# Sums of the first norm in the transposes' PSUM banks, six projections in six banks, and the relative bias by one product of eight rows with copies in DRAM

## The chip, the cores and the metric

The kernel runs on one core of a Trainium2 chip. The metric is the device time of one execution in microseconds (us), from launch to end, as the median of several runs. The engines work in parallel, each through its own queue in a fixed order: TensorE (PE; PEld is its weight load), VectorE (DVE), ScalarE (ACT), GpSimd (POOL) and SyncE (SP), which issues the DMAs.

## The reference

A two-layer decoder trunk on 1024 tokens of width 1024, all in float32. Layer 0 is a mixer with two groups of heads, layer 1 is latent attention; a SwiGLU FFN follows each. The change lies in layer 0, whose core is:

```python
h = rmsnorm(x, attn_norm[0])                 # y * rsqrt(mean(y*y) + eps) * gain
proj = h @ w_in                              # q_a, k_a, v_a (8 heads), q_b (8), k_b, v_b (2)
# group A, stick-breaking attention: weights are products of (1 - sigmoid) over the keys between
# group B, window of 128 keys:
rel = BLOCK + arange(BLOCK)[:, None] - arange(2 * BLOCK)[None, :]
bias = rel_bias_table[t5_bucket(rel)]        # 32 buckets x 8 heads, the same for every block
logits = where(valid, q_b @ k_b.T * d ** -0.5 + bias, -inf)
p = exp(logits - m); p = p / (sum(p) + exp(sink - m))
x = x + concat([o_a, o_b]) @ w_out
```

## The kernel before

Activations lie transposed (channels on the 128 partitions, tokens along the row) in two halves of 512 tokens. Every float32 matrix operand is split into a rounded part and its rest (`whi`, `wlo` for weights, `hh`, `hl` for the normed input), and each product is made of three passes (`mm3`, L237 to L239): `whi*hh`, `whi*hl`, `wlo*hh`. One projection of one half is 8 k-steps, so 24 products of 128x512, collected in one PSUM bank.

PSUM has eight banks. In this stage they are four tags of two: `mm` (projections), `z` (scores), `t` (transposes) and `o` (attention outputs).

The stage begins with `norm_in` (L353): it loads the 16 tiles of x, splits them (`hh` on ACT, L311; `hl` on DVE, L312), squares them and adds the squares up in two tiles for each half (L270 to L277). The two are added on DVE (`merge`, L910), and a product with a matrix of ones (L285 in `rstd`) sums over the partitions. Then ACT takes Ln and Exp (L289, L296; each needs its table loaded) and DVE makes three steps (L297 to L299) to the scale `r` of that half. The projections don't wait for `r`: it is multiplied in when a bank is emptied (`evac`, L514).

Then come the first six projections by a loop in `layer0_attention`: k, q and v of the first pair of heads, both halves each, in the order k half 0, q half 0, k half 1, q half 1, v half 0, v half 1. An emptied q or k is split again for the scores (casts on ACT, L522, L531, L532; subtractions of 64x512 on POOL, L523, L533, L534; q takes two subtractions, k four). An emptied v is differenced (DVE L657, L659, POOL L655), transposed (PE L370) and split (ACT L376, DVE L377).

After them `weave` lays the rest out by hand for PE: eight segments (four pairs of stick-breaking heads, then four pairs of windowed heads). Each is a list of steps (transposes L706, values L719, scores L686, two slots ahead), and each carries fillers: the projections of a later segment, cut in pieces of two k-steps. The fillers' declared weights set the pace: after slot i of n, the share i/(n-1) of the whole weight should have run. Segment 3's fillers are the bias (`bias_items`), then k, one q and v of the windowed heads.

Up to the first segment the program's order on every engine, and in the whole program the order on DVE, ACT, POOL and SP, is chosen by a scheduler at build time that replays the program with modelled times; a change at one place can so change the order at another.

The bias: for each of the eight heads DVE spreads the head's column of the table over 128 columns (L435), PE multiplies it with a one-hot matrix of 33x384 in float32 (L436), which gives the head's row of 384 biases on all 128 partitions, ACT copies it out (L438), and SP stores it to DRAM (L439). There it is read back with a row step one element shorter (L581), which shifts each row by one, into the tile that L596 adds to the scores.

Of the kernel before, what the change touches and what calls it, by code (L numbers as in the profile page):

```python
# [10 lines left out]
F32 = mybir.dt.float32  # L11
# [4 lines left out]
ALU = mybir.AluOpType  # L16
# [4 lines left out]
P = 128  # L21
D = 1024
# [3 lines left out]
HALF = 512  # L26
# [3 lines left out]
WLEN = 384  # L30
# [33 lines left out]
def once(fn):  # L64
    def g():
        fn()
        return
        yield
    return g


class Kernel:
# [203 lines left out]
        eng = nc.gpsimd if k in (2, 4) else nc.vector  # L276
        eng.tensor_tensor(accs[k % 2], accs[k % 2], out, ALU.add)  # L277

    def rstd(self, r, accs, n, scale=1.0, eps=None, eps_out=None):


        nc, dv = self.nc, self.nc.vector
        ps = self.bank("mm")
        for i, acc in enumerate(accs):
            nc.tensor.matmul(ps, self.ones, acc, start=i == 0, stop=i == len(accs) - 1)  # L285
        v = self.tmp("nv")
        t = self.tmp("nt")
        if eps is None:
            nc.scalar.activation(t, ps, AF.Ln, scale=1.0 / n, bias=self.eps)  # L289
            dv.tensor_scalar(v, ps, 1.0 / n, EPS, ALU.mult, ALU.add)  # L290
        else:
            dv.scalar_tensor_tensor(v, ps, 1.0 / n, eps, ALU.mult, ALU.add)
            nc.scalar.activation(t, v, AF.Ln)
        if eps_out is not None:
            dv.tensor_scalar(eps_out, ps, EPS / n, EPS * EPS, ALU.mult, ALU.add)
        nc.scalar.activation(r, t, AF.Exp, scale=-0.5, bias=self.log_q if scale != 1.0 else 0.0)  # L296
        dv.tensor_tensor(t, r, r, ALU.mult)  # L297
        dv.scalar_tensor_tensor(t, t, -0.5 / scale ** 2, v, ALU.mult, ALU.mult)
        dv.scalar_tensor_tensor(r, t, 1.5, r, ALU.add, ALU.mult)  # L299
        return r  # L300
# [46 lines left out]
    def norm_in(self, xsrc, g0, pool, tag, split=False, hook=None):  # L347
        act = [[None, None] for _ in range(NT)]
        rs = []
        for hf in range(2):  # L350
            accs = []
            srcs = []
            for k in range(NT):  # L353
                if hook:
                    hook(k, hf)
                srcs.append(xsrc(k, hf))
                act[k][hf] = self.split_act(srcs[k], k, hf, g0 + k)
                if not split:
                    self.stat_acc(accs, srcs[k], k)
            if split:  # L360
                for k in range(NT):
                    self.stat_acc(accs, srcs[k], k)
            rs.append(self.rstd(self.tl(pool, [P, HALF], F32, tag, 2), self.merge(accs), D))
        return act, rs

    def v_tokens(self, fv, hf, v):
# [51 lines left out]
    def bias_items(self):  # L418

        nc, a = self.nc, self.a
        box = {}

        def start():
            t = self.tl(self.atp, [P, 514], F32, "w", self.nw)
            box["oh"], box["tab"] = t[:33, :WLEN], t[:33, WLEN:WLEN + 8]
            nc.sync.dma_start(out=box["oh"], in_=a["c_onehot"])
            nc.sync.dma_start(out=box["tab"][:32], in_=a["rel_bias_table"])
            nc.vector.memset(box["tab"][32:33], 1.0)  # L430

        def rows(h):
            ps = self.bank("mm")
            lhs = self.tl(self.atp, [P, HALF], F32, "u", 3)[:33, :P]
            nc.vector.tensor_scalar(lhs, self.ones[:33], box["tab"][:, h:h + 1], None, ALU.mult)  # L435
            nc.tensor.matmul(ps[:, :WLEN], lhs, box["oh"], start=True, stop=True)  # L436
            t = self.tl(self.atp, [P, HALF], F32, "ev", 2)
            nc.scalar.copy(t[:, :WLEN], ps[:, :WLEN])  # L438
            nc.sync.dma_start(out=self.dram("bias", h, width=WLEN + 1)[:, :WLEN], in_=t[:, :WLEN])  # L439

        return [(0, once(start))] + [(1, once(lambda h=h: rows(h))) for h in range(8)]

    def drive(self, segments):

# [124 lines left out]
    def swa_steps(self, mi, kbox, vbox, qbox, done):  # L569
        nc = self.nc  # L570
        g = mi // 2
        box = {}

        def score(b):
            if b % 4 == 0:
                box["s", b // 4] = self.tl(self.atp, [P, 2, 4], F32, "sum", 3)
            if b == 0:
                box["b"] = self.tl(self.atp, [P, HALF], F32, "u", 3)
                for h in range(2):
                    rows = self.dram("bias", 2 * mi + h, width=WLEN + 1)  # L580
                    nc.sync.dma_start(out=box["b"][:, 256 * h:256 * h + 256],  # L581
                                      in_=bass.AP(rows.tensor, rows.offset + P - 1, [[WLEN, P], [1, 256]]))
            bias = box["b"].rearrange("p (h k) -> p h k", h=2)
            khs, kls = kbox["t"]
            kh, kl, qs = khs[g], kls[g], qbox["t"]
            z = self.bank("z")
            zv = z.rearrange("p (h k) -> p h k", h=2)
            o = P if b == NB - 1 else 0
            for h in range(2):
                for i, k in enumerate((kh, kl)):  # L590
                    nc.tensor.matmul(zv[:, h, :], qs[h][:, b * P:(b + 1) * P],
                                     k[:, b * P - o:b * P - o + 256], start=i == 0, stop=i == 1)
            pt = self.tl(self.atp, [P, 2, 257], F32, "w", self.nw)
            st = self.tl(self.atp, [P, 2], F32, "sst", 6)
            nc.gpsimd.tensor_copy(pt[:, :, 256], self.sinks[:, 2 * mi:2 * mi + 2])
            nc.vector.scalar_tensor_tensor(pt[:, :, o:256], zv[:, :, o:], 0.125, bias[:, :, :256 - o],  # L596
                                           ALU.mult, ALU.add)
            nc.vector.tensor_reduce(st, pt[:, :, o:], AX.X, ALU.max, negate=True)
            for h in range(2):
                nc.scalar.activation(pt[:, h, o:], pt[:, h, o:], AF.Exp, bias=st[:, h:h + 1],  # L600
                                     accum_out=box["s", b // 4][:, h, b % 4:b % 4 + 1])
            box["p", b] = pt, o
# [16 lines left out]
        def pv(b, nk, hi, lo):  # L619
# [15 lines left out]
            if b % 4 == 3:  # L635
                hf = b // 4
                self.normalise(box["s", hf].rearrange("p h b -> p (h b)"), hf, ot, "u", 3)
                done(hf, ot)

        return [([(0, lambda b=b: score(b))], [lambda b=b: part(b)], None) for b in range(NB)]  # L640

    def sb_values(self, fv, hf, box):
# [114 lines left out]
    def layer0_attention(self):  # L757
        nc, a = self.nc, self.a
# [3 lines left out]
        with self.pool("at") as self.atp, self.pool("ps", space=PSUM) as self.ps:  # L762
# [39 lines left out]
            def q_tiles(i):  # L802
                if i < 2:
                    qt.append(self.qk_tiles(2))
                return qt[i % 2]

            qs = [self.unit_items(self.stack_q, lambda i=i: q_tiles(i)) for i in range(4)]
            for i, tag in ((0, "z"), (2, "mm"), (1, "z"), (3, "mm"), (4, "z"), (5, "mm")):
                self.dtag = tag
                for _ in sb[0][0][i][1]():  # L810
                    pass
# [906 lines left out]
```

## Time and profile before

| what | us |
|---|---|
| median of 3 runs (lowest to highest) | 2478.38 (2477.58 to 2479.45) |
| the profiled execution | 2477.88 |
| its span, first to last instruction | 2476.1 |
| PE busy | 2320.3 (94%) |
| DVE busy | 1914.9 (77%) |
| ACT busy | 1232.4 (50%) |
| POOL busy | 970.2 (39%) |

1.8 us of the profiled execution lie around the span. PE is busy nearly all the time, but a busy PE can run at two clocks (1.2 and 2.4 GHz), which the column PEclk of the view by windows shows as a share of the higher. In a timeline a row gives its start, its duration, the engine, the line, what it writes and reads, and in brackets the engine's idle time before it and what ended that.

### The profile page before, as it was taken

Reading aid. Unit: us, or ns where it says so; the run is one execution under the profiler, and the core shown is the slowest. Engines: PE = TensorE matmul, PEld = TensorE weight load, DVE = VectorE, ACT = ScalarE, POOL = GpSimd, SP = SyncE. Lnnn points to the kernel's source line nnn. Section 1 sums busy time; section 2 is a strip of 40 time slices with the busy share of each in tenths; the row PEclk is TensorE's granted clock in tenths of the full one; section 3 lists DMA queues with packets and bytes.
Section 4 is the critical chain, followed back from the end, with each engine's and each line's share of the span. In section 5 each row is a group of like instructions: output and inputs, shape, how many; then the busy total and the mean of one; then the engine's idle time right before and its main releaser. Section 6 shows DMA issues by size and latency. Waiting matters only on the chain. (4 is left out here: it accounts for less than half of the span.)

```text
span 2476.1 us, 33778 instructions
## 1 busy us (share of the span) xinstructions
PE 2320.3 (94%) x11252; PEld 1907.3 (77%) x11252; DVE 1914.9 (77%) x2864; ACT 1232.4 (50%) x2469; POOL 970.2 (39%) x786
## 2 busy tenths in 40 slices
PE   7999998889999999999987999999989999999996
PEld 5777787777788888778766888887768888887784
DVE  6787776778577678899987888885587776678988
ACT  6555565645223334344665788775453223243453
POOL 5333232213977443433222323321135564434333
PEclk8999999999999999999998999999999999999998
DMA  3011125644445335453343111135334443355531
GB/s 121 26 44 39 65 95 183 200 162 145 132 158 177 100 111 170 145 173 125 112 127 96 50 62 62 52 118 204 100 106 166 162 153 106 116 159 156 170 104 71
DMA packets 167114, 298.64 MB, mean 121 GB/s; under 512 B 20667, under 2 KB 29340, under 8 KB 166940
## 3 DMA queue, kind: packets, MB, share of 16 engines
q1 hardware_dynamic: 166940, 296.49, 36.7%
q8 instruction: 88, 1.44, 0.2%
q14 instruction: 86, 0.70, 0.1%
HBM read 214.53 MB, written 81.36 MB: 119 GB/s over the span
## 5 line engine op out<-in xcount | busy, mean ns | idle before, releaser
L145 ACT CAST whi<-wa 128x512 fp32r<-128x512 f32 (+1 forms) x422 | 255.7, 607 | 457.4 <-PE mm L238 111.9
L146 DVE TENSOR_TENSOR wlo<-wa,whi 128x512 fp32r<-128x512 f32 (+1 forms) x422 | 343.2, 814 | 75.4 <-ACT whi L145 73.5
L178 POOL TENSOR_TENSOR wa<-s,wa 128x512 f32<-128x512 f32 (+1 forms) x66 | 94.3, 1428 | 255.4 <-DVE wlo L146 227.3
L201 POOL TENSOR_TENSOR s<-wb,wb 128x512 f32<-128x512 f32 (+1 forms) x66 | 93.6, 1418 | 203.9 <-DVE wlo L146 149.9
L1470 PE MATMUL z<-mk,mq 128*128 128x512 f32 (+2 forms) x576 | 148.8, 369 | 10.1 <-ACT w L1483 9.4
L146 DVE TENSOR_TENSOR wlo<-wb,whi 128x512 fp32r<-128x512 f32 (+1 forms) x136 | 135.6, 997 | 25.8 <-ACT whi L145 25.7
L145 ACT CAST whi<-wb 128x512 fp32r<-128x512 f32 (+1 forms) x136 | 82.3, 605 | 141.6 <-PE d L238 44.6
L237 PE MATMUL mm<-hh,whi 128*128 128x512 f32 x312 | 128.5, 412 | 1.6 <-ACT whi L145 1.6
L1483 ACT ACTIVATE w<-z,st 128x512 f32<-128x512 f32 (+3 forms) x192 | 110.7, 582 | 32.5 <-DVE st L1479 23.2
L1476 DVE TENSOR_REDUCE st<-z 128x1 f32<-128x512 f32 (+1 forms) x192 | 104.2, 549 | 28.9 <-PE z L1470 19.9
L238 PE MATMUL mm<-hl,whi 128*128 128x512 f32 x312 | 125.3, 402 | 0.0
L239 PE MATMUL mm<-hh,wlo 128*128 128x512 f32 x312 | 124.8, 400 | 0.0
L178 POOL TENSOR_TENSOR wa<-wa,wa 128x512 f32<-128x512 f32 (+1 forms) x68 | 105.3, 1549 | 43.9 <-issue 26.8
L398 DVE TENSOR_TENSOR ptl<-t,pth 128x512 fp32r<-128x512 f32 x160 | 108.0, 682 | 13.3 <-ACT pth L397 10.7
L934 POOL TENSOR_TENSOR c<-c,c 128x512 f32<-128x512 f32 x66 | 101.6, 1554 | 26.0 <-DVE c L1052 22.7
L1470 PEld LDWEIGHTS z<-mk,mq 128*128 128x128 f32 x576 | 93.6, 193 | 23.3 <-ACT w L1483 14.6
L178 POOL TENSOR_TENSOR wb<-wa,wb 128x512 f32<-128x512 f32 (+1 forms) x68 | 100.1, 1472 | 27.0 <-DMA wa<-w_gate 23.1
L397 ACT CAST pth<-t 128x512 fp32r<-128x512 f32 x160 | 90.6, 591 | 17.3 <-PE t L394 7.5
L394 PE MATMUL t<-ident,w 128*128 128x128 f32 x576 | 95.0, 277 | 1.3 <-ACT w L1483 1.2
L402 PE MATMUL mm<-pth,v 128*128 128x256 f32 x320 | 93.5, 309 | 1.4 <-ACT pth L397 1.2
L402 PE MATMUL mm<-ptl,v 128*128 128x256 f32 x320 | 87.8, 298 | 2.4 <-DVE ptl L398 2.0
L710 DVE TENSOR_TENSOR ptl<-t,pth 128x512 fp32r<-128x512 f32 x80 | 54.4, 683 | 40.6 <-ACT pth L709 40.2
(530 smaller groups left out, 7613.3 us busy)
## 6 DMA issues: line engine op xcount, KB each, us to landing
a<-c SPq DMA_DIRECT2D x120, 256.0 KB, 3.1
ld<-a SPq DMA_DIRECT2D x98, 256.0 KB, 3.6
wa<-w_gate SPq DMA_DIRECT2D x68, 256.0 KB, 2.6
wa<-w_up SPq DMA_DIRECT2D x68, 256.0 KB, 2.7
lone<-a SPq DMA_DIRECT2D x56, 256.0 KB, 3.4
wb<-w_gate SPq DMA_DIRECT2D x44, 256.0 KB, 3.2
wb<-w_up SPq DMA_DIRECT2D x44, 256.0 KB, 2.7
wa<-w_in SPq DMA_DIRECT2D x36, 256.0 KB, 2.7
```

The lines of the kernel that those rows point to most:

```text
L145: nc.scalar.copy(hi[:, :n], raw[:, :n])
L146: nc.vector.tensor_tensor(lo[:, :n], raw[:, :n], f(hi[:, :n]), ALU.subtract)
L178: sub = lambda o, x, y: nc.gpsimd.tensor_tensor(o, x, y, ALU.subtract)
L237: mm(ps, wh, xh, start=first, stop=False)
L238: mm(ps, wh, xl, start=False, stop=False)
L239: mm(ps, wl, xh, start=False, stop=last)
L398: nc.vector.tensor_tensor(lo, t, f(hi), ALU.subtract)
L402: nc.tensor.matmul(o[:, :256], vs, pt[:, j * 256:(j + 1) * 256], start=(kb == kb0 and j == 0 and i == 0), stop=(kb == NB - 2 and j == 1 an ...
L934: sub = lambda o, x, y: nc.gpsimd.tensor_tensor(o, x, y, ALU.subtract)
L1470: nc.tensor.matmul(z[:, :wd + ext], qq[:, q0:q0 + P], kk[:, k0 - ext:k0 + wd], start=y == 0, stop=y == 2 and x > 0)
L1476: nc.vector.tensor_reduce(st[:, x:x + 1], zs[x], AX.X, ALU.max, negate=True)
L1483: nc.scalar.activation(w[:, o:o + wd], zs[x], AF.Exp, bias=st[:, 2 * np_ - 2:2 * np_ - 1], accum_out=box[p]["s"][c // 2][:, 8 * x + j:8 * ...
```

## The change

Four things are changed in layer 0. The sums of the first norm go to a bank of tag `t` instead of `mm`, and the two tiles of squares aren't added on DVE first: both go through the product with ones. Of the six first projections the last two (v) go to the banks `o`, where before v half 0 took a `z` bank and v half 1 an `mm` bank. The bias of all eight heads is made by one product, with the table itself as the stationary operand, as eight rows of 384; those go to DRAM, and eight DMAs from DRAM to DRAM spread one row each over 128 rows. The rows are read back as before. The bias is now one filler of declared weight 1 with a pause inside, where before it was a start of weight 0 and eight of weight 1.

```diff
-    def rstd(self, r, accs, n, scale=1.0, eps=None, eps_out=None):
+    def rstd(self, r, accs, n, scale=1.0, eps=None, eps_out=None, tag="mm"):
-        ps = self.bank("mm")
+        ps = self.bank(tag)
...
-            rs.append(self.rstd(self.tl(pool, [P, HALF], F32, tag, 2), self.merge(accs), D))
+            rs.append(self.rstd(self.tl(pool, [P, HALF], F32, tag, 2), accs if split else self.merge(accs), D,
+                                tag="t" if split else "mm"))
...
+        def rows():
             t = self.tl(self.atp, [P, 514], F32, "w", self.nw)
+            oh, tab = t[:33, :WLEN], t[:33, WLEN:WLEN + 8]
+            nc.sync.dma_start(out=oh, in_=a["c_onehot"])
+            nc.sync.dma_start(out=tab[:32], in_=a["rel_bias_table"])
+            nc.vector.memset(tab[32:33], 1.0)
+            yield
             ps = self.bank("mm")
+            nc.tensor.matmul(ps[:8, :WLEN], tab, oh, start=True, stop=True)
             t = self.tl(self.atp, [P, HALF], F32, "ev", 2)
+            nc.scalar.copy(t[:8, :WLEN], ps[:8, :WLEN])
+            rows = self.drp.tile([8, WLEN], F32, name=self.nm("bias"))
+            nc.sync.dma_start(out=rows, in_=t[:8, :WLEN])
+            self.bias = self.drp.tile([8, P, WLEN + 1], F32, name=self.nm("bias"))
+            for h in range(8):
+                nc.sync.dma_start(out=self.bias[h, :, :WLEN],
+                                  in_=bass.AP(rows.tensor, rows.offset + h * WLEN, [[0, P], [1, WLEN]]))
-        return [(0, once(start))] + [(1, once(lambda h=h: rows(h))) for h in range(8)]
+        return [(1, rows)]
...
-            for i, tag in ((0, "z"), (2, "mm"), (1, "z"), (3, "mm"), (4, "z"), (5, "mm")):
+            for i, tag in ((0, "z"), (2, "mm"), (1, "z"), (3, "mm"), (4, "o"), (5, "o")):
```

The change moves instructions at three places that the prediction speaks of. The first is PE at the end of the first norm. In the names, `z104` is the bank of k half 0, `mm114` of q half 0, `z116` of k half 1, `mm118` of q half 1; `mm97` and `t55` are banks of the norm's sums, `w46`, `w47` and `w88` tiles of squares. PE before, where the second half's sum stands:

```order
L237 MATMUL z116_372<-hh7_186_247,whi32_129 128x512
L238 MATMUL z116_372<-hl7_187_248,whi32_129 128x512
L239 MATMUL z116_372<-hh7_186_247,wlo33_130 128x512
L285 MATMUL mm97_275<-w88_251,ones3_62 128x512
L237 MATMUL mm114_341<-hh0_020_105,whi59_193 128x512
L238 MATMUL mm114_341<-hl0_021_106,whi59_193 128x512
```

PE now, from the last product that has its old place:

```order
L237 MATMUL z104_292<-hh7_044_153,whi32_129 128x512
L237 MATMUL mm114_341<-hh0_020_105,whi59_193 128x512
L238 MATMUL mm114_341<-hl0_021_106,whi59_193 128x512
L285 MATMUL t55_180<-w46_157,ones3_62 128x512
L237 MATMUL z116_372<-hh0_162_199,whi17_99 128x512
L237 MATMUL mm118_407<-hh0_162_199,whi59_193 128x512
L285 MATMUL t55_180<-w47_159,ones3_62 128x512
L238 MATMUL z104_292<-hl7_045_154,whi32_129 128x512
L239 MATMUL z104_292<-hh7_044_153,wlo33_130 128x512
L239 MATMUL mm114_341<-hh0_020_105,wlo60_194 128x512
```

Before, q half 0 stood behind the sum of the second half; now it is woven with k half 0, k half 1 and q half 1, and the sum of the second half (`t97`) comes 68 rows later than `t55`, between the last products of q half 1 and the first of v.

The second place is ACT around the second half's Ln (L289). ACT before (`ev105` is k half 0, `ev115` q half 0, `ev117` k half 1, emptied):

```order
L532 CAST qk100_288<-ev105_317 64x512
L531 CAST qk101_289<-ev105_317 64x512
L532 CAST qk101_289<-ev105_317 64x512
L289 ACT_TABLE_LOAD
L289 ACTIVATE w99_278<-mm97_275,eps7_70 128x512
L296 ACT_TABLE_LOAD
L296 ACTIVATE r096_273<-w99_278 128x512
L522 CAST qk112_339<-ev115_366 64x512
```

ACT now:

```order
L145 CAST whi110_335<-wa109_333 128x512
L524 CAST qk112_339<-ev115_366 64x512
L524 CAST qk113_340<-ev115_366 64x512
L145 CAST whi121_440<-wa120_438 128x512
L145 CAST whi124_446<-wa123_444 128x512
L289 ACT_TABLE_LOAD
L289 ACTIVATE w99_278<-t97_274,eps7_70 128x512
L296 ACT_TABLE_LOAD
L296 ACTIVATE r096_273<-w99_278 128x512
L533 CAST qk100_288<-ev117_397 64x512
```

The split of q half 0 has moved ahead of the second half's Ln, and with it four casts of later weights; the tag `whi` has four buffers, so `whi124` takes that of `whi68`, which the last product of q half 1 reads.

The third place is PE in segment 3. PE before, in the slots after the first pair of bias products (`o` values, `t` transposes, `z` scores):

```order
L686 MATMUL z_2750<-qk_1996,qk_2225 128x384
L686 MATMUL z_2750<-qk_1998,qk_2225 128x384
L436 MATMUL mm_2756<-w_2700,u_2757 128x384
L436 MATMUL mm_2764<-w_2700,u_2765 128x384
L719 MATMUL o_2772<-pth_2696,v_2436 128x256
```

PE now:

```order
L433 MATMUL mm_2704<-w_2700 8x384
L721 MATMUL o_2643<-pth_2653,v_1720 128x256
L721 MATMUL o_2643<-ptl_2654,v_1720 128x256
L721 MATMUL o_2643<-pth_2653,v_1720 128x256
L721 MATMUL o_2643<-ptl_2654,v_1720 128x256
```

Of eight bias products one is left (8x384), and the projections of k, q and v begin two slots after it and are spread over the whole segment, where before they began behind the eighth bias product. Beyond this the scheduler's order differs at a few rows near 490 us and, with the same instructions, in the first pairs of layer 1's attention (some 1315 to 1440 us in the trace of before).

## Rows read from the trace of the kernel before

**Rows 1.** The page's head and its first part: the span, and PE's busy time, share of the span and count.

```profile
span 2476.1 us, 33778 instructions
PE 2320.3 (94%) x11252; PEld 1907.3 (77%) x11252; DVE 1914.9 (77%) x2864; ACT 1232.4 (50%) x2469; POOL 970.2 (39%) x786
```

**Rows 2.** PE's waits from 0 to 72 us: what waited, on what, us in total, times, longest.

```profile
PE mm L285 <- DVE w L910: 7.7, 1, 7.7
...
PE t L706 <- DVE v L377: 3.3, 1, 3.3
PE z L686 <- ACT w L688: 1.4, 1, 1.4
```

**Rows 3.** Timelines of PE, ACT and DVE from 18 to 49 us, single rows in order of time: start us, duration us, engine, line, operation, out<-in, shapes, and in brackets the idle time before it.

```profile
19.68 0.72 PE L237 MATMUL z<-hh,whi 128*128 128x512 f32 x2
...
38.32 0.68 DVE L514 TENSOR_TENSOR ev<-z,r 128x512 f32<-128x512 f32 x1
...
38.45 2.08 PE L285 MATMUL mm<-w,ones 128*128 128x512 f32 x2 [7.65 <-DVE w L910]
39.54 1.42 PE L237 MATMUL mm<-hh,whi 128*128 128x512 f32 x1
...
41.58 1.28 ACT L289 ACT_TABLE_LOAD   x1
42.87 0.69 ACT L289 ACTIVATE w<-mm,eps 128x512 f32<-128x512 f32 x1
...
44.87 0.63 ACT L296 ACTIVATE r<-w 128x512 f32<-128x512 f32 x1
...
46.99 0.69 DVE L299 SCALAR_TENSOR_TENSOR r<-w,r 128x512 f32<-128x512 f32 x1
...
48.22 0.68 DVE L514 TENSOR_TENSOR ev<-z,r 128x512 f32<-128x512 f32 x1
```

**Rows 4.** Timeline of POOL from 28 to 80 us: the subtractions of k half 0, q half 0, and the first and last row of k half 1 and q half 1.

```profile
39.73 1.26 POOL L533 TENSOR_TENSOR qk<-ev,qk 64x512 fp32r<-64x512 f32 x1 [4.28 <-ACT qk L531]
...
49.04 2.66 POOL L523 TENSOR_TENSOR qk<-ev,qk 64x512 fp32r<-64x512 f32 x2 [4.05 <-ACT qk L522]
51.77 1.29 POOL L533 TENSOR_TENSOR qk<-ev,qk 64x512 fp32r<-64x512 f32 x1
...
57.88 2.65 POOL L523 TENSOR_TENSOR qk<-ev,qk 64x512 fp32r<-64x512 f32 x2
```

**Rows 5.** Timelines of PE and DVE from 52 to 72 us: the first and last product of v half 0, the first scores, the first transposes of segment 0, and the emptying of v half 1.

```profile
52.86 0.39 PE L237 MATMUL z<-hh,whi 128*128 128x512 f32 x1
...
58.07 0.39 PE L239 MATMUL z<-hh,wlo 128*128 128x512 f32 x1
...
63.75 0.63 PE L686 MATMUL z<-qk,qk 128*128 128x256 f32 x4
...
71.14 0.45 PE L706 MATMUL t<-ident,w 128*128 128x128 f32 x1 [3.32 <-DVE v L377]
...
64.00 0.69 DVE L514 TENSOR_TENSOR ev<-mm,r 128x512 f32<-128x512 f32 x1 [1.66 <-PE mm L239]
```

**Rows 6.** Busy time by windows: the window, then its length, busy us (and count) of PE, PEld, DVE, ACT, POOL; then PEclk, the share of the DMA engines, GB/s.

```profile
24.00:27.00 3.00, 3.00 (x7) 1.67 (x6) 3.00 (x6) 1.24 (x2) 0.00 (x0) 0.55 0.35 113
27.00:31.00 4.00, 3.80 (x17) 2.82 (x15) 4.00 (x7) 3.14 (x6) 0.00 (x0) 1.00 0.04 6
...
38.40:43.70 5.30, 5.25 (x10) 3.52 (x11) 0.71 (x2) 4.56 (x7) 3.80 (x3) 0.50 0.00 0
43.70:52.80 9.10, 9.10 (x41) 7.51 (x40) 3.88 (x6) 6.11 (x9) 4.90 (x4) 1.00 0.01 2
```

**Rows 7.** Timeline of DVE from 12 to 40 us: the same subtraction of a weight, once beside a square on POOL, once alone.

```profile
13.86 1.52 DVE L146 TENSOR_TENSOR wlo<-wa,whi 128x512 fp32r<-128x512 f32 x1
...
23.92 0.68 DVE L146 TENSOR_TENSOR wlo<-wa,whi 128x512 fp32r<-128x512 f32 x1
```

**Rows 8.** Timeline of PE from 272 to 300 us, the rows of the bias products (two records a product), and two of PE's waits from 272 to 345 us.

```profile
275.95 2.93 PE L436 MATMUL mm<-w,u 33*128 33x384 f32 x4
...
282.20 1.79 PE L436 MATMUL mm<-w,u 33*128 33x384 f32 x4
...
285.02 1.55 PE L436 MATMUL mm<-w,u 33*128 33x384 f32 x4
...
288.43 0.91 PE L436 MATMUL mm<-w,u 33*128 33x384 f32 x2
...
290.38 0.91 PE L436 MATMUL mm<-w,u 33*128 33x384 f32 x2
...
PE t L706 <- DVE w L690: 1.6, 1, 1.6
PE t L562 <- DVE ev L514: 1.3, 1, 1.3
```

**Rows 9.** The views by line of L439 (the time to landing of its eight DMAs of 128x384), L581 and L596: line, engine, operation, count, then ns min/median/max, first and last start in us, forms.

```profile
DMA to landing us min/median/max: 2.1/2.4/2.6
...
L581 SPq DMA_DIRECT2D u<-bias x8: 319/430/587, 286.6 to 459.9; - x8
...
L596 DVE SCALAR_TENSOR_TENSOR w<-z,u x32: 426/693/694, 344.8 to 488.6; 128x512 f32<-128x512 f32 x28, 128x256 f32<-128x256 f32 x4
```

**Rows 10.** PE's longest wait from 1300 to 1440 us, in the first pairs of layer 1's attention.

```profile
PE z L1470 <- ACT w L1483: 7.6, 4, 3.4
```

More of the change, by code (lines that the diff above doesn't have):

```diff
@@ L422, in bias_items @@
         nc, a = self.nc, self.a
-        box = {}
-        def start():
+        def rows():
             t = self.tl(self.atp, [P, 514], F32, "w", self.nw)
[L427 to L432, printed above, removed]
+            oh, tab = t[:33, :WLEN], t[:33, WLEN:WLEN + 8]
[3 more added lines that the diff above has]
+            yield
             ps = self.bank("mm")
-            lhs = self.tl(self.atp, [P, HALF], F32, "u", 3)[:33, :P]
-            nc.vector.tensor_scalar(lhs, self.ones[:33], box["tab"][:, h:h + 1], None, ALU.mult)
-            nc.tensor.matmul(ps[:, :WLEN], lhs, box["oh"], start=True, stop=True)
+            nc.tensor.matmul(ps[:8, :WLEN], tab, oh, start=True, stop=True)
             t = self.tl(self.atp, [P, HALF], F32, "ev", 2)
-            nc.scalar.copy(t[:, :WLEN], ps[:, :WLEN])
-            nc.sync.dma_start(out=self.dram("bias", h, width=WLEN + 1)[:, :WLEN], in_=t[:, :WLEN])
-        return [(0, once(start))] + [(1, once(lambda h=h: rows(h))) for h in range(8)]
+            nc.scalar.copy(t[:8, :WLEN], ps[:8, :WLEN])
[6 more added lines that the diff above has]
+        return [(1, rows)]
     def drive(self, segments):
@@ L579, in score @@
                 for h in range(2):
-                    rows = self.dram("bias", 2 * mi + h, width=WLEN + 1)
                     nc.sync.dma_start(out=box["b"][:, 256 * h:256 * h + 256],
-                                      in_=bass.AP(rows.tensor, rows.offset + P - 1, [[WLEN, P], [1, 256]]))
+                                      in_=bass.AP(self.bias.tensor, self.bias.offset + (2 * mi + h) * P * (WLEN + 1) + P - 1,
+                                                  [[WLEN, P], [1, 256]]))
             bias = box["b"].rearrange("p (h k) -> p h k", h=2)
```

## The prediction

> **What bounds the kernel now.** I read the page's busy times first: PE is busy 2320.3 of 2476.1 us, 94% [rows 1], so time can come only from work that PE no longer does where it is full, or from the few places where PE waits. Hence the view of PE's waits at the start, where three of the four edits lie: its longest is L285, 7.7 us for `merge` on DVE [rows 2]. The timelines around it [rows 3] show the chain behind: PE has had nothing to do since 38.45 - 7.65 = 30.80, DVE is late with the squares, and the sum of the second half starts at 38.45. From there nothing is parallel: table and Ln on ACT from 41.58, table and Exp until 45.50, three steps on DVE until 47.68, k half 1 emptied until 48.90, then the splits on POOL, which POOL takes one after another until 60.53 [rows 4], and the first scores at 63.75 [rows 5]. The windows show a second price of the wait: in the 5.3 us after it PE's clock is 0.50, thereafter 1.00 [rows 6]. So POOL's splits of k half 1 and q half 1 release the first scores, and they wait for the second half's scale.
>
> Last I read PE around segment 3: busy without a gap worth naming, apart from 1.6 and 1.3 us of transposes waiting, and the bias products stand in the middle of it [rows 8].
>
> **The start: 6.8 us, the likeliest gain.** With the sums in a bank of their own tag, PE need not hold q half 0 back. By the order it has issued 22 of the four projections' 96 products when it comes to the row at 19.68 [rows 3]; 74 are left. A product at full clock takes (58.07 - 52.86)/23 = 0.227 us [rows 5], so 16.8. Three products with ones (two for the first half, the first for the second) stand among them; one takes 39.54 - 38.45 = 1.09 [rows 3], so 3.3. From 19.7, with 0.4 for the last to drain, they end at 19.7 + 16.8 + 3.3 + 0.4 = 40.2. The squares of the second half were ready at 38.45 minus a merge, so the sum follows at once and DVE no longer sets it.
>
> Then the old chain, with durations of [rows 3]. On ACT stand a cast of a weight that waits for the last product of q half 1 (0.6, taken as Exp's on the same 128x512), table 1.28, Ln 0.69, table 1.28, Exp 0.63: 4.5, to 44.7. From the end of Exp (45.50) to the end of L299 (47.68) it took 2.2: to 46.9. Emptying k half 1 adds 0.7: 47.6, against 48.90 before. ACT's cast of it takes 0.6, so POOL begins at 48.2. It needs 60.53 - 51.77 = 8.8 for k half 1 and q half 1 [rows 4]: the first scores at 57.0, against 63.75. The larger part of the gain is thus not the 1.3 us by which the scale comes sooner: before, q half 0's 2.66 on POOL (49.04) stood ahead of k half 1 [rows 4], since q half 0 was computed behind the sum; now it is done before the scale is there. PE still has 48 products of v and one with ones in that time, 48 x 0.227 + 1.1 = 12.0, so it is through at 52.2, 4.8 us ahead of the scores, and POOL is the bound. What is late next is v half 1, emptied beside the first scores as before (64.00 [rows 5]). From the first scores to the first transposes 7.4 us pass (63.75 to 71.14 [rows 5]), and I leave them.
>
> The v banks themselves cost nothing I can find: a bank of `o` is first wanted by the values of segment 0, behind the transposes at 71.14; its cover is some 10 us after PE's 52.2. The merges that go (two on DVE) stood in front of the wait and are in the 7.7. The two products with ones that are new cost 2.2 and are in the sum above.
>
> Bounds: 74 products at the low clock (0.50 from 38.4 to 43.7 [rows 6]) would take twice as long, 33.6 instead of 16.8: scores at 73.8, 10.1 later than before. Of lower prices, a stretch like that from 24 to 27 us, granted 0.55 after PE had waited [rows 6], costs 3.0 x 0.45 = 1.4. At best the chain from scores to transposes also shortens by its 3.3 us wait for v [rows 2], and the gain is 9 to 10.
>
> A rule speaks against this term. The row first: the subtraction L146 of a weight takes 1.52 us beside a square on POOL and 0.68 alone [rows 7]. The Trainium skill (GPSIMD Engine Reference, section 1, Specifications) has GpSimd share SBUF interfaces with VectorE, and lose to contention where a VectorE instruction has two SBUF inputs; the trace agrees. Now k half 0's and q half 0's splits on POOL fall beside four weight subtractions and the last squares on DVE: by the rule 5 x 0.84 = 4.2 us more on DVE, of which I reckon that at most 2 reach the second half's sum, and the total would be 2 us higher.
>
> **The bias: 4.8 us.** The records of L436 add up to 2.93 + 1.79 + 1.55 + 0.91 + 0.91 = 8.09 us, two to a product, so seven products are 7.1 of it; at full clock one is 0.91 [rows 8]. I take seven at 0.91 as removed, 6.4. Against it one new wait like the 1.6 us of transposes for DVE [rows 8], since PE comes sooner to the same scans: 6.4 - 1.6 = 4.8. Nothing of the 8 steps on DVE and ACT counts, since PE doesn't wait for them except through the products. Bounds: zero, if what PE gains is lost at the next waits for DVE or ACT; 7.1 + 1.6 + 1.3 = 10, if waits vanish too.
>
> The eight copies from DRAM to DRAM, 196,608 bytes each, 1.57 MB in all, are in no row. The nearest are the eight stores of L439, which land 2.1 to 2.6 us after issue [rows 9]. One after another that would be 19 us. They are wanted when the loads L581 run ahead of the first L596, at 344.8 before and some 12 us sooner now, 333; the store before them comes with the product, near 270. So some 60 us cover them, and I cost them at nothing. All DMAs are issued by SP, in order: the first bias load waits for its copy, and behind it stand the weights of segments 4 on. If the cover is gone, PE waits for L596 and for those weights.
>
> By a page alone: the Trainium skill (DMA: Bandwidth & Descriptors, Anatomy of one DMA — SWDGE (gpsimd) path) fits 2.0 us and the bytes at 436 GB/s, on another path of issue; its estimate is 3.6 + 2.0 us, no run here shows it, and the sum would be the same.
>
> The even spread of segment 3's projections moves PE work within the segment and adds none: zero, inside the bounds above.
>
> **The reordered rows.** Near 490 us a few rows change places, and from 1315 to 1440 us whole pairs do, with the same instructions. PE's wait there is 7.6 us in four [rows 10], so one wait more or fewer is 1.9, two are 3.8. No row says which way: zero, plus or minus 3.8.
>
> **Sum.** 6.8 + 4.8 + 0 = 11.6. The profiled execution took 2477.88, its span 2476.1 and 1.8 around it, 0.5 below the median of 2478.38. So 2477.88 - 11.6 = 2466.3, and 2466.8 as a median.
>
> **Rivals.** Main case, 0.66: both gains come; 2466.8, of its own 2461 to 2472 (the reorder's 3.8, and 1 to 2 for the clock or POOL).
>
> The bias gain is hidden, 0.20: PE finds itself ahead of scans and softmax and waits there. For it: PE's waits before L706 [rows 8] all end on DVE. Against it: they are 2.9 us in 73. 2478.4 - 6.8 = 2471.6.
>
> The low clock holds through the start, 0.10: the woven products have gaps in them, and the clock stays at half. For it: PE busy 1.00 of the time at 0.55 from 24 to 27 us, and 0.50 after the long wait [rows 6]. Against it: the weave gives PE work that doesn't wait. The start would cost 10.1 instead of gaining 6.8: 2478.4 + 10.1 - 4.8 = 2483.7 at its worst; with half of the 74 products so, 8.4 of the 16.8 come on top, 2466.8 + 8.4 = 2475.2.
>
> Slower, 0.04: the copies hold SP. If 1.57 MB take more than about 60 us (25 GB/s), L596 waits for the bias and the weights behind it in SP's queue come late; the first 12 us of that only eat the gain, so it decides from about 73 us, 21 GB/s. At 78 us, 18 are lost: 2466.8 + 18 = 2484.8. For it: one row of 1536 bytes is read 128 times from DRAM. Against it: 2.4 us for as many bytes stored [rows 9].
>
> **Range and chances.** 2459 (both gains at their better bounds, with the reorder's) to 2477 (bias hidden, a low stretch, and the reorder against it). 0.2% is 5 us, about what a measurement of this kernel tells from no change: faster below 2473.4. All of the main case but a tenth, and most of the hidden one are faster, with some of the low clock: 0.78; the same 0.15; slower, from the worst of the low clock, of the copies and of the reorder, 0.07.
>
> **What would show it.** PE's wait at L285 for L910 is gone, and PE at 1.00 from 27 us until the v products end near 52; the first scores stand at 57, the first transposes of segment 0 near 64. POOL does q half 0 before k half 1. One L433 of about 0.9 us stands where eight L436 stood, and L596 starts near 333. The waits of layer 1 from 1300 to 1440 us stay near 7.6. I am wrong on the start if the scores come later than 62 with POOL idle before them or PE at 0.50 after 30; on the bias if PE's waits from 272 to the first L596 grow by more than 3; on the copies if L596 waits for a bias load longer than for any other.

## The result and the profile after

| what | us |
|---|---|
| before, median of 6 runs (lowest to highest) | 2478.82 (2477.58 to 2482.59) |
| after, median of 6 runs (lowest to highest) | 2466.96 (2461.47 to 2467.82) |
| ratio, with its 95% interval | 0.9948 (0.9935 to 0.9962) |
| after, the profiled execution and its span | 2461.47, 2459.7 |
| PE busy in it | 2311.8 (94%) |

The kernel became 11.9 us faster, where 11.6 were forecast. The profiled execution is the fastest of the six, 5.5 us below their median, so its end says less than its single stages; those are read here, and the same kernel was profiled once more below.

The start first. PE's waits from 0 to 72 us after the change, to be held against [rows 2]:

```profile
PE z L237 <- ACT hh L311: 6.0, 1, 6.0
PE z L688 <- POOL qk L525: 4.8, 1, 4.8
PE z L238 <- DVE hl L312: 3.8, 3, 2.0
PE t L708 <- DVE v L378: 1.2, 1, 1.2
```

The 7.7 us for `merge` are gone. In their place PE waits 4.8 us at the first scores, and what it waits for is the first of POOL's two last splits (L525). The timeline of PE after, single rows: the four sums, the last product of v half 1, the first scores, the first transposes of segment 0.

```profile
20.27 1.33 PE L285 MATMUL t<-w,ones 128*128 128x512 f32 x2
...
21.91 1.02 PE L285 MATMUL t<-w,ones 128*128 128x512 f32 x2
...
36.87 1.02 PE L285 MATMUL t<-w,ones 128*128 128x512 f32 x2
...
39.82 1.02 PE L285 MATMUL t<-w,ones 128*128 128x512 f32 x2
...
51.15 0.39 PE L239 MATMUL o<-hh,wlo 128*128 128x512 f32 x1
56.33 3.34 PE L688 MATMUL z<-qk,qk 128*128 128x256 f32 x8 [4.79 <-POOL qk L525]
...
64.11 0.45 PE L708 MATMUL t<-ident,w 128*128 128x128 f32 x1 [1.24 <-DVE v L378]
```

Against [rows 3] and [rows 5]: the last sum ran at 39.82 (the products ahead of it were put to end at 40.2), PE was through with v at 51.5 (52.2), the first scores stand at 56.33 (57.0; before 63.75) and the first transposes at 64.11 (64; before 71.14).

The scale itself came no sooner. DVE's timeline after, the first and last step of the scale (L297, L299) and the emptying of k half 1:

```profile
44.84 1.51 DVE L297 TENSOR_TENSOR w<-r 128x512 f32<-128x512 f32 x1 [0.96 <-ACT r L296]
...
47.11 0.69 DVE L299 SCALAR_TENSOR_TENSOR r<-w,r 128x512 f32<-128x512 f32 x1
47.90 0.69 DVE L516 TENSOR_TENSOR ev<-z,r 128x512 f32<-128x512 f32 x1
```

L299 ends at 47.80, in [rows 3] it ended at 47.68; 46.9 was put. Nearly all of these 0.9 us are L297's: it took 1.51 us beside POOL's split of q half 0 (42.80 to 45.79, below), where it had taken 0.69 before, with POOL idle. So what held the scores back in the kernel before? The view by windows of before, the stretch in front of them:

```profile
60.00:63.70 3.70, 3.70 (x18) 3.08 (x17) 0.69 (x1) 0.63 (x1) 1.71 (x3) 1.00 0.09 18
```

PE was busy all of it with the last products of v, while POOL had been done with its splits since 60.53 [rows 4]. Before, it was PE's own queue that stood in front of the first scores, late by the wait of 7.65 us and the low clock behind it; after, PE is through at 51.5 and POOL's splits stand there.

The clock, in the view by windows of after, answers to [rows 6]:

```profile
24.00:27.00 3.00, 3.00 (x15) 2.47 (x14) 3.00 (x6) 2.97 (x5) 0.00 (x0) 1.00 0.26 87
...
31.00:43.00 12.00, 12.00 (x51) 9.18 (x50) 11.16 (x10) 8.14 (x14) 9.17 (x7) 1.00 0.19 51
43.00:52.00 9.00, 8.54 (x38) 6.75 (x36) 5.06 (x7) 5.05 (x8) 5.29 (x4) 1.00 0.15 52
52.00:58.00 6.00, 1.62 (x5) 1.33 (x6) 2.97 (x4) 3.53 (x6) 5.74 (x4) 0.75 0.18 49
```

PE is busy without a gap from 24 to 51.5 us and the clock is 1.00 all the time; it falls only with the wait at the scores. POOL's timeline after is the chain that sets the scores, and shows the price of working beside DVE:

```profile
36.05 1.60 POOL L535 TENSOR_TENSOR qk<-ev,qk 64x512 fp32r<-64x512 f32 x1 [2.50 <-ACT qk L533]
37.71 1.64 POOL L536 TENSOR_TENSOR qk<-ev,qk 64x512 fp32r<-64x512 f32 x1
...
42.80 2.99 POOL L525 TENSOR_TENSOR qk<-ev,qk 64x512 fp32r<-64x512 f32 x2
49.33 1.29 POOL L535 TENSOR_TENSOR qk<-ev,qk 64x512 fp32r<-64x512 f32 x1 [3.53 <-ACT qk L533]
...
55.02 2.94 POOL L525 TENSOR_TENSOR qk<-ev,qk 64x512 fp32r<-64x512 f32 x2
```

q half 0 is split (42.80) ahead of k half 1 (49.33), as the sum had it; in [rows 4] it stood in front of it at 49.04. A subtraction takes 1.60 to 1.64 while DVE works beside it and 1.29 alone.

Segment 3 next. One and the same row of DVE near the segment's end, the rest of the windowed heads' values, bounds it. Before and after:

```profile
339.79 0.69 DVE L567 TENSOR_TENSOR v<-t,v 128x512 fp32r<-128x512 f32 x1 [1.37 <-ACT v L566]
```

```profile
327.34 0.67 DVE L569 TENSOR_TENSOR v<-t,v 128x512 fp32r<-128x512 f32 x1
```

That is 12.45 us sooner. At 247.41 before, a scan on DVE ahead of segment 3, the distance was 5.47, so the stretch between gained 7.0. PE's bias products in that stretch by the view by line, before and after (two records a product):

```profile
L436 PE MATMUL mm<-w,u 33*128 33x384 f32 x16 | 8.1, 624 | 0.0
```

```profile
L433 PE MATMUL mm<-w 33*8 33x384 f32 x2 | 1.4, 825 | 0.0
```

6.7 us of products are gone. And PE's waits in the stretch, before and after:

```profile
PE t L706 <- DVE v L377: 2.7, 1, 2.7
PE t L706 <- DVE w L690: 1.6, 1, 1.6
PE t L562 <- DVE ev L514: 1.3, 1, 1.3
...
PE t L370 <- DVE u L657: 0.6, 1, 0.6
```

```profile
PE t L708 <- DVE v L378: 2.3, 1, 2.3
PE z L688 <- ACT w L690: 1.9, 1, 1.9
PE t L371 <- POOL u L657: 0.6, 1, 0.6
PE t L371 <- DVE u L659: 0.6, 1, 0.6
```

The waits of 1.6 and 1.3 (both in [rows 8]) are gone, one of 1.9 for ACT is new: with the line left out (POOL, 0.6) the sums are 6.8 and 5.4. From there to the end the distance goes from 12.5 to 16.4 in this execution, in steps of one to three us up and down; the second profile below shows what to make of them.

The copies, SP's timeline of after: the store of the rows, the eight copies, the first two bias loads.

```profile
272.10 0.28 SPq L437 DMA_DIRECT2D bias<-ev  x1
273.52 5.05 SPq L440 DMA_DIRECT2D bias<-bias  x8
...
280.48 1.03 SPq L582 DMA_DIRECT2D u<-bias  x2
```

The loads go out at 280.48 and the first L598 stands at 330.36, 50 us later.

### The profile page after: what moved, and what is told of

Same layout as the page of the kernel before. It is cut to its first block, busy times and chain, and to the rows that moved or that the text cites. A ratio compares the mean times of both kernels' runs of the same rounds, so it can differ in the third digit from the quotient of the medians.

```text
span 2459.7 us, 33726 instructions
## 1 busy us (share of the span) xinstructions
PE 2311.8 (94%) x11242; PEld 1901.9 (77%) x11242; DVE 1916.6 (78%) x2854; ACT 1229.4 (50%) x2462; POOL 975.7 (40%) x786
## 5 line engine op out<-in xcount | busy, mean ns | idle before, releaser
L1485 ACT ACTIVATE w<-z,st 128x512 f32<-128x512 f32 (+3 forms) x192 | 110.7, 582 | 35.2 <-DVE st L1481 25.3
```

The lines of the kernel that those rows point to most:

```text
L1485: nc.scalar.activation(w[:, o:o + wd], zs[x], AF.Exp, bias=st[:, 2 * np_ - 2:2 * np_ - 1], accum_out=box[p]["s"][c // 2][:, 8 * x + j:8 * ...
```

## The experiments

Each kernel ran in five or more rounds beside runs of the kernel before on the same chip. Their medians for before were 2480.55 (first four), 2481.45 (next four) and 2481.26 (last three), some 2 us above the first chip, so only differences to these are compared. The executions of one kernel lie 5 to 14 us apart; where it drowns what an experiment asks, the stage in the trace decides.

### The changed kernel again, and its two halves

c0_after is the changed kernel, unedited.

> The changed kernel again, nothing edited, to tell how far its executions and its profile scatter: the profiled execution took 2461.5 us, where the median of six was 2467.0. If the medians are the thing to explain, this comes to 2465 to 2468 and its median gain over the kernel before is 11 to 12.5 us. If instead the low profile shows a better course that the kernel takes often, the median falls to 2463 or less.

Measured: 2465.66 (2461.18 to 2467.86), 14.9 under before, ratio 0.9937 (0.9925 to 0.9950). The median of after stands; its gain is larger here since before is slower. The stages come out as in the first profile: first scores 56.57, first transposes 64.34, and the DVE row that stands at 339.79 before is 13.8 us sooner, at 325.98. From there to the end the distance goes from 13.8 to 13.2, not up to 16.4: what comes behind segment 3 has no sign of its own. The stretch of layer 1 whose rows change places [rows 10] hardly matters: from 1320 to 1456 us of before the distance went from 17.0 to 17.4 in the first profile of after, and from 14.6 to 15.0 in this one.

e1_start has the edits of the start alone:

```diff
-    def rstd(self, r, accs, n, scale=1.0, eps=None, eps_out=None):
+    def rstd(self, r, accs, n, scale=1.0, eps=None, eps_out=None, tag="mm"):
...
-            for i, tag in ((0, "z"), (2, "mm"), (1, "z"), (3, "mm"), (4, "z"), (5, "mm")):
+            for i, tag in ((0, "z"), (2, "mm"), (1, "z"), (3, "mm"), (4, "o"), (5, "o")):
```

> Only the edits of the start: the sums in the t banks without the merge, v in the o banks; the bias as before. Theory (the start's gain is its own, 6.8 forecast, 6.5 in the trace of after): 6 to 7 us under the kernel before, scores at about 57.6 us. Rival (a sooner start only brings the later stages to the same DMAs and waits, so that it is given back): 0 to 3 under it, though the first scores are sooner.

Measured: 2469.87, 10.7 under before, ratio 0.9953 (0.9941 to 0.9966). In its trace the scores stand at 56.08 and the transposes at 63.84. At 308.56 us before, behind the bias products, it was 5.3 ahead, so the start gives 5 to 7 us at its stage and has kept them there; at the end its trace is 8.0 ahead of that of before, so 2.7 came behind that stage. The rest of the 10.7 is that before is slower on this chip than in its trace (2480.55 beside 2477.88).

e2_bias has the edit of the bias alone, `rstd`, `norm_in` and the six banks being those of before.

> Only the edit of the bias; the start as before, with PE's wait of 7.7 us for the merge. Theory (seven products of 0.91 us leave a full PE, less one wait): 4 to 7 us under the kernel before. Rival 1 (hidden: PE comes sooner to waits for scans and softmax): 0 to 2. Rival 2 (the parts only gain together): e1 and e2 together fall short of the 12 us of both by 3 or more.

Measured: 2476.22, 4.3 under before, ratio 0.9982 (0.9973 to 0.9991). The stage: 0.37 us behind before at 242.80, 6.62 ahead at 339.79, so 7.0 again. 10.7 + 4.3 = 15.0, beside 14.9 for both at once: the two halves add up, and rival 2, a shortfall of 3 or more, does not show. But what the medians split as 10.7 and 4.3 the stages split as 5.3 to 6.8 and 7.0. By their intervals the medians allow 8.4 to 14.6 and 2.2 to 6.7, so the stage's figures lie outside: something behind the stage, or in the course of before on this chip, adds to the one half and takes from the other, and which is not shown.

### The bias: products, pace and copies

e3_eight issues the one product eight times:

```diff
-            nc.tensor.matmul(ps[:8, :WLEN], tab, oh, start=True, stop=True)
+            for _ in range(8):
+                nc.tensor.matmul(ps[:8, :WLEN], tab, oh, start=True, stop=True)
```

> The changed kernel with its one bias product issued eight times into the same bank, the result the same: seven products of 8x384 more on PE, at the same place, with the new spread of the projections, the one copy and the DMAs from DRAM to DRAM kept. Theory (the bias gain is PE time): 6 to 7 us over the changed kernel, so nearly all the gain of the bias given back. Rival (the gain comes from the evenly spread projections, or from the 8 steps on DVE and ACT that are gone): 0 to 3 us over it.

Measured: 2476.95, 11.3 over the changed kernel of the same job; ratio to before 0.9989 (0.9980 to 0.9998). More than either theory put. Its rows say why, by PE's timeline and by the windows around it:

```profile
270.54 10.40 PE L434 MATMUL mm<-w 33*8 33x384 f32 x16
280.88 0.58 PE L722 MATMUL o<-pth,v 128*128 128x256 f32 x1
```

```profile
270.50:280.80 10.30, 10.30 (x18) 1.96 (x16) 0.69 (x1) 0.58 (x1) 0.00 (x0) 0.50 0.01 2
280.80:284.00 3.20, 3.20 (x13) 2.87 (x13) 1.07 (x3) 1.89 (x5) 0.00 (x0) 0.50 0.02 4
```

(280.88 - 270.54) / 8 = 1.29 us a product, at 0.50, against 0.91 at full clock in [rows 8]: seven cost 9.1. The same row of DVE as above stands at 337.37, 11.4 behind c0_after's 325.98; of that 1.8 was there at 247 already. So PE time it is: the rival of 0 to 3 falls, and the size of the theory was off mainly by the clock.

e8_oldpace keeps the single product and lets the projections of segment 3 begin later, nearly as late as before (at 281.49, where c0_after has 273.20):

```diff
+            for _ in range(7):
+                yield
...
-        return [(1, rows)]
+        return [(8, rows)]
```

> The changed kernel, with the declared weight of the bias at 8 in place of 1, so that the projections of segment 3 begin some five slots later, about as before the change; the same instructions. Prediction as put (moving the projections within the segment costs nothing): 0 to 1 us over the changed kernel, and all of the 7 us at segment 3 comes from the seven products. Rival (the slots that the products left need the projections, else PE waits there for scans): PE's waits between 255 and 335 us grow by 2 to 6 us, and so does the time.

Measured: 2464.75, ratio 0.9936 (0.9919 to 0.9954); at the start of segment 4 its trace is 0.9 us ahead of c0_after (at 342 us), with PE's waits in segment 3 at 5.3 us. The rival falls. By the medians the even spread neither gave nor cost; by the stage it cost 1.1, since this trace was still 0.3 behind c0_after at 247 us. In c0_after the clock behind the bias product is low for a while, and six products of a projection stand in that stretch (273.20 to 275.76); here values and transposes stand there. The window of c0_after:

```profile
270.00:276.00 6.00, 6.00 (x21) 5.17 (x21) 4.08 (x6) 2.92 (x6) 1.80 (x1) 0.52 0.26 73
```

e7_copies issues the copies eight times over:

```diff
-            for h in range(8):
+            for h in list(range(8)) * 8:
```

> The changed kernel with the eight copies from DRAM to DRAM issued eight times over, 64 in place of 8. In the trace of after SP issues one in 0.64 us, and the loads of the bias follow 2.5 us after the last. Theory (the copies stand beside other work with some 50 us to spare): SP is held for 36 us more, the first loads of the bias land near 320 where the first L598 stands at 330, and the time is 0 to 2 us over the changed kernel. Rival (the weights behind them in SP's queue were already wanted then, or the copies disturb each other): 5 us or more over it, with PE waiting for projections in segment 3.

Measured: 2482.24, 1.0 over before, where c0_after is 14.9 under it; ratio 1.0007 (0.9996 to 1.0017). The theory's 0 to 2 over the changed kernel is missed; the rival has the size, but not the place: up to 340 us PE's waits are those of after, 5.4. SP's and PE's timelines, and DVE's waits from 320 to 345 us:

```profile
273.68 63.25 SPq L440 DMA_DIRECT2D bias<-bias  x64
...
338.10 1.10 SPq L582 DMA_DIRECT2D u<-bias  x2
```

```profile
DVE w L598 <- DMA u<-bias: 13.3, 1, 13.3
```

```profile
349.27 1.11 PE L564 MATMUL t<-ident,ev 128*128 128x128 f32 x4 [13.38 <-DVE ev L516]
```

A copy held SP 63.25/64 = 0.99 us in such a row, not 5.05/8 = 0.63, so the loads went out at 338.10 in place of 280.48. DVE waits 13.3 us at L598, and behind it in DVE's queue stands the emptying of a projection (L516), for which PE waits 13.4. The slower rival of the prediction is thus a real mechanism, and the slack that the eight copies leave is measured: the loads went out 57.6 us later and L598 waited 13.3, so some 44 us were free.

### The start: the merge, the bank, the v banks, POOL

e4_merge puts the merges back and leaves the sums in the `t` banks; e6_summm leaves the merges out and puts the sums back into the `mm` banks; e5_vbanks puts v into `z` and `mm`.

```diff
-            rs.append(self.rstd(self.tl(pool, [P, HALF], F32, tag, 2), accs if split else self.merge(accs), D,
+            rs.append(self.rstd(self.tl(pool, [P, HALF], F32, tag, 2), self.merge(accs), D,
```

> The changed kernel with the two merges on DVE put back in front of the sums; the sums stay in the t banks, so that the projections of q half 0 need not stand behind the second half's sum. Theory (the bank is what counts, since PE has projections to run while DVE adds; the first scores wait for POOL's splits): 0 to 2 us over the changed kernel, first scores by 59.5 us. Rival (the merge is what counts, being late on DVE): 5 to 7 us over it, PE waiting at L285 again.

```diff
-                                tag="t" if split else "mm"))
+                                tag="mm"))
```

> The changed kernel with the sums back in the mm banks but without the merge. Theory (the bank is what counts: q half 0 stands behind the second half's sum again, and its split comes ahead of k half 1's on POOL): 4 to 7 us over the changed kernel, first scores at 62 to 64 us, and PE waiting at L285, now for the squares themselves. Rival (the merge): 0 to 2 us over it.

```diff
-            for i, tag in ((0, "z"), (2, "mm"), (1, "z"), (3, "mm"), (4, "o"), (5, "o")):
+            for i, tag in ((0, "z"), (2, "mm"), (1, "z"), (3, "mm"), (4, "z"), (5, "mm")):
```

> The changed kernel with v half 0 and v half 1 back in a z and an mm bank. Every engine keeps its order. Theory (nothing: in the trace of after v begins at 39.6 us, k half 0 and q half 0 were emptied at 35.9): first scores within 0.5 us of 56.6, the time within the scatter of the changed kernel, 0 to 1. Rival (v in the mm or z bank holds back the first scores or segment 0's first projection): 2 us or more over it at the first transposes.

| kernel | median | ratio to before | first scores | first transposes |
|---|---|---|---|---|
| before | | | 63.75 | 71.14 |
| c0_after | 2465.66 | 0.9937 (0.9925 to 0.9950) | 56.57 | 64.34 |
| e4_merge | 2468.92 | 0.9955 (0.9940 to 0.9971) | 58.95 | 66.83 |
| e6_summm | 2467.93 | 0.9948 (0.9936 to 0.9960) | 60.58 | 68.35 |
| e5_vbanks | 2466.44 | 0.9944 (0.9930 to 0.9958) | 56.54 | 64.31 |
| v2_dve | 2464.76 | 0.9936 (0.9922 to 0.9950) | 54.63 | 63.32 |

The v banks are worth nothing, as put: 0.03 us at the transposes. Of the 6.8 us at the transposes the merge put back takes 2.5 and the bank put back 4.0. Neither theory is wholly right: the bank is the larger part, yet without the merge the old bank alone loses by the median less than its price of 4 to 7, and with the merge the sum in the new bank still waits for it. The sum of e4_merge on PE; then, of e6_summm, PE's first product of v and its sum of the second half, and POOL's rows:

```profile
43.42 1.13 PE L285 MATMUL t<-w,ones 128*128 128x512 f32 x2 [1.86 <-DVE w L912]
```

```profile
28.51 0.39 PE L237 MATMUL o<-hh,whi 128*128 128x512 f32 x1
...
41.45 1.02 PE L285 MATMUL mm<-w,ones 128*128 128x512 f32 x2
```

```profile
50.44 2.66 POOL L525 TENSOR_TENSOR qk<-ev,qk 64x512 fp32r<-64x512 f32 x2 [6.78 <-ACT qk L524]
53.18 1.29 POOL L535 TENSOR_TENSOR qk<-ev,qk 64x512 fp32r<-64x512 f32 x1
...
59.26 2.94 POOL L525 TENSOR_TENSOR qk<-ev,qk 64x512 fp32r<-64x512 f32 x2
```

With the merge, PE has used up its projections and waits 1.86 us for L912; on DVE that merge took 1.75 us beside POOL's splits (0.68 without, in the trace of before). With the `mm` banks the theory had PE wait at L285; it doesn't, but q half 0's 2.66 us stand in front of k half 1 again on POOL. PE doesn't wait because 33 products of v now run ahead of that sum (28.51 to 41.45): v has banks of its own, which this edit leaves in `o`. So that the v banks are worth nothing is shown only with the sums in `t`, and what the old bank costs with v in `z` and `mm` too, as before the change, was not run. At 247 us e4_merge is 4.4 us ahead of before and e6_summm 0.2, where the seven traces with the whole new start lie 5.0 to 6.8 ahead: there the bank's part stands clear of the scatter, the merge's hardly. By the medians c0_after, e4_merge and e6_summm lie within their intervals of each other; what is shown is shown by the stage.

v2_dve gives three of POOL's six last subtractions to DVE:

```diff
-            nc.gpsimd.tensor_tensor(kls[h][l, c], src[m, :], f(khs[h][m, c]), ALU.subtract)
+            (nc.vector if self.boot and hf and h else nc.gpsimd).tensor_tensor(kls[h][l, c], src[m, :], f(khs[h][m, c]), ALU.subtract)
```

(and in the same way one of q and the other of k, for the first six projections alone)

> The changed kernel with three of the six subtractions of k half 1 and q half 1 of the first pair on DVE in place of POOL. Theory (the first scores wait for POOL's splits and nothing else: POOL was busy with them from 49.33 to 57.96 in the trace of after, PE through with v at 51.4): the scores come 3 to 4 us sooner, and the kernel is 2 to 4 us under the changed one. Rival (the next wait, for v half 1, stands right behind): 0 to 1.

The first scores come 1.9 us sooner, where 3 to 4 were put, the transposes 1.0, and at 92 us nothing is left of it. The rival holds: POOL's splits release the scores, but v half 1 is late right behind.

### A version that beats both

In the trace of after DVE waits for the bias loads of the later pairs. These loads stand in SP's queue behind a store and a read-back (L333, L337) that end the pair before. v1_prebias loads the next pair's bias in the middle of a pair:

```diff
-            if b == 0:
-                box["b"] = self.tl(self.atp, [P, HALF], F32, "u", 3)
+            if b in (0, 4) and mi + b // 4 < 4 and mi + b // 4 not in self.bt:
+                m = mi + b // 4
+                self.bt[m] = self.tl(self.atp, [P, HALF], F32, "u", 3)
...
```

> The changed kernel with the bias of the next pair of windowed heads loaded in the middle of a pair, not at the head of its own. In the trace of after DVE waits three times at L598 for that load, 13.6 us, and PE behind it at L613. If these waits stand on the path: 6 to 12 us under the changed kernel. If they only stand in front of others (PE's work there ends at the same weights or values): 0 to 3 under it.

Measured: 2458.43 (2457.36 to 2462.79), 23.0 under before, ratio 0.9916 (0.9904 to 0.9927), beside 14.9 and 0.9937 for the changed kernel. DVE's longest waits in segments 4 on, of c0_after (331 to 486 us) and of this kernel (332 to 478):

```profile
DVE w L598 <- DMA u<-bias: 15.2, 3, 7.1
DVE o L635 <- ACT otmp L633: 12.3, 7, 4.4
```

```profile
DVE wlo L146 <- ACT whi L145: 12.3, 7, 5.2
DVE o L638 <- ACT otmp L636: 7.0, 7, 1.6
```

The wait for the load is gone, and DVE waits in its place for casts of weights. From the third row of the bias addition (L598, 337.20 in c0_after; L601, 338.71 here) to an addition of the output projection (491.60 and 483.90) it is 9.2 us shorter. PE's idle time in that stretch falls by 6.5 us, and its busy time by 2.7, at a granted clock of 0.98 in place of 0.93. So the waits stood on the path, and some of the gain is clock that came with fewer waits.

## Why the prediction was right, point by point

- **The start, 6.8.** Right in size, at the upper end: 7.0 in the first profile of after and 6.8 in c0_after at the first transposes; at 247 us 5.5 and 6.8, and 5.0 to 6.6 in the five other traces with the whole new start. Its steps came within about 1 us: the scale 0.9 later than put (47.8 for 46.9), POOL's start 1.1 later (49.33 for 48.2), and the scores yet 0.7 sooner, since they begin when the first of the two L525 is done and not the second. Two small errors cancel on the way to the last sum: a product with ones costs 0.87 us at full clock (36.87 to 37.97 after, less one product of 0.227) and not the 1.09 read from a row at the clock of 0.50, and the first of them stood at 20.27, 0.6 after the 19.7 put.
- **What bounded the start before** is where the prediction read wrong. It said that POOL's splits release the first scores; before, they were done 3.2 us earlier, and PE's own products of v stood in front. The sum came out because after the change it is POOL, as it had worked out. Where the gain lies is therefore told another way: the change takes PE from the bound, and POOL's new order (q half 0 ahead of the scale) keeps the next bound low. The scale coming 1.3 us sooner, which it also counted, did not happen; k half 1 was emptied 0.3 sooner (48.59 for 48.90).
- **The bank or the merge.** The bank put back costs 4.0 at the transposes, the merge put back 2.5, each with the v banks new. The sentence that DVE "no longer sets" the sum holds only without the merge: put back, it makes PE wait 1.86 us.
- **The rule against it (VectorE and GpSimd beside each other).** The slowing is there, 1.6 against 1.29 us on POOL and 1.51 against 0.69 on DVE. In front of the second half's sum DVE had the time: its last square ended at 38.20, and PE came to the sum at 39.82. So the hedge of 2 us was not needed there. Behind the sum it did cost: L297 stands in the chain to the scale, and its 0.8 us are nearly all of the 0.9 by which the scale came late.
- **The low clock through the start** (rival): no. PE ran from 24 to 51.5 us at 1.00.
- **The bias, 4.8.** Right in mechanism, wrong in size: the term "minus one wait like the 1.6 us" was the mis-sized one. Segment 3 gained 7.0 in all of three profiles (after, c0_after, e2_bias): 6.7 of products, and waits that fell by 1.4 in place of rising by 1.6, less about 1.1. That last part, which the prediction left out, is most likely six products of a projection that now run at the low clock behind the bias product (273.20 to 275.76 in c0_after, 2.56 us for 6 x 0.227 = 1.36); e8_oldpace, with values and transposes in that place, has a stage shorter by 1.1. That the bias gain might be hidden (the rival at 0.20) falls by e3_eight.
- **The spread of the projections, 0.** Right by the medians; at the stage it cost the 1.1 us that e8_oldpace gets back.
- **The copies, 0 with some 60 us of cover.** Right. From the store (272.10) to the first L598 (330.36) pass 58 us, as put; the copies and the loads use some 14 of them, and 44 are left. A copy lands 5.6 to 7.1 us after its issue in c0_after, over twice the stores of [rows 9], but they overlap: from the first issue (272.0) to the last landing (276.5 and 7.1 at most) pass no more than 11.6 us, below the 19 put as a bound. The sign that was to speak against this term, L596 waiting longest for a bias load, was ill chosen: that wait is there after the change (13.6 us in three), but it was there before (14.4 in three), and it is for the loads of later pairs, which don't stand behind the copies.
- **The reordered rows, 0 plus or minus 3.8.** Right: 0.4 in both profiles, toward faster. PE's waits for L1485 there are 8.6 us in six, where 7.6 in four were to stay.
- **The sum.** By the stages it is 12.5 and 13.8 at the end of segment 3, 1 to 2 us more than the 11.6 put; the medians gave 11.9 and 14.9. That 2466.8 met 2466.96 so closely is luck of a us or two: executions of one kernel differ by more, and a bias gain 2.2 over the forecast stood against a start that in most traces fell 1 to 2 short of it.
- **The range.** Its lower end, 2459, was said to hold the better bounds of both gains and the reorder's 3.8; by the prediction's own terms the two bounds alone give it, and with the 3.8 it would be 2455. The measured time lies far from either.

## What to carry to other kernels

Before a wait is priced, look which engine is busy right up to the instruction that matters: here the first scores stood behind PE's own queue, and the wait of 7.7 us counted only until POOL's splits became the next bound. Price a small float32 product by its time on PE at the clock that holds there, not by its rows: at 0.50 one with 8 rows took 1.29 us, one with 128 rows 2.93/2 = 1.47 [rows 8]. Where an engine waits for a load, look whether SP holds that load behind another transfer, and issue it a stage sooner.

## What the runs showed of the hardware beyond that

- Eight float32 products of 33x8 by 384 in a row keep PE busy for 10.3 us without a gap, and the clock stays at 0.50 all through them: a busy PE isn't a PE at full clock. With one such product the low stretch behind the wait ended by 276 us, with eight by 284.
- Copies from DRAM to DRAM of one row to 128 cost SP 0.63 us each to issue as eight and 0.99 as 64 in a row, and the 64 landed 4.9 to 11.1 us after issue.
- Executions of the same kernel differ by the clock behind the same waits. From one row of DVE to another (129.7 and 160.3 us of before), after and c0_after run the same 146 records on PE and have the same waits (2.3, 0.6, 0.6 and 0.6 us), yet after takes 31.46 us at a granted clock of 0.89 and c0_after 30.59 at 0.94. Such a step of 0.9 us is one part of the scatter seen here, and most of the difference between their 5.5 and 6.8 at 247 us; why the clock comes back sooner in one execution than in another is not shown.
